# Raw weight chunks from the common pool of 8 KB units, in a hybrid decoder layer

## The chip, the cores and the metric

The kernel runs on one core of one Trainium2 chip. Its time is device time in microseconds (us), the median of several runs. Five engines work beside each other, each on its own list of instructions in a fixed order: TensorE (PE) for matmuls and transposes, VectorE (DVE), ScalarE (ACT), GpSimd (POOL), and SyncE (SP), which here only issues DMAs. They wait for each other through semaphores. "PEld" in the profile is TensorE's loading of weights, "PEclk" the clock that TensorE was granted, as a share of full speed.

## The reference

One decoder layer on x of 512 x 1024, everything in float32: a mixer with dilated attention (8 heads) and retention (4 heads) side by side, cross attention to 256 memory rows (4 heads), and SwiGLU. Each part is normed ahead and behind and added to x:

```
y = hybrid_mixer(rms_norm(x, pre_mix_g), w_in, attn_gn_g, ret_gn_g, w_out)
x = x + rms_norm(y, post_mix_g)
y = memory_cross_attn(rms_norm(x, pre_mem_g), mem, mem_norm_g, w_q, w_kv, w_o)
x = x + rms_norm(y, post_mem_g)
y = swiglu(rms_norm(x, pre_ffn_g), w_gate_up, w_down)
x = x + rms_norm(y, post_ffn_g)
```

where `rms_norm(x, g) = x * rsqrt(mean(x*x) + 1e-6) * g`, row by row. All the projections together read some 80 MB of weights.

## The kernel before

**Three matmuls for one.** A float32 product is computed from a high and a low half of each operand (`mm3`, L84 to L86): high by high, high by low, low by high. A weight therefore passes through four steps, in `load` (from L101): SP issues the DMA of a raw chunk of 128 x 2048 floats (8 KB in each partition, 1 MB in all; L109), ScalarE rounds it to the high half `wh` (L90), VectorE subtracts to get the low half `wl` (L91), each in two pieces of 1024 columns; then TensorE may use it. The tile names in the profile are `raw`, `wh`, `wl`. `split` does the same with activations.

**Chunks in a fixed sequence.** `chunks` lists all weight chunks in the order of use; `take` hands one out and calls `load` for those up to two ahead. For the mixer's output projection (`w_out`) and for the query projection of the cross attention (`w_q`) all four chunks are taken before the loop that uses them.

**Buffers.** `up` is a pool of 20 units of 8 KB (in each partition), all with one tag: the halves of weights, the transposed activations, queries, keys, values and x itself come from it through `unit` and `pair`. A new unit waits until the unit whose place it takes has had its last reader. `rawp` is a pool of two more units of 8 KB, for raw chunks alone, and for two landings of the memory input (`memTr`, L514, and `mrow`, L523): the third raw chunk waits until the first has been read out by ScalarE and VectorE. Gains that are multiplied along a row (`load_gain`, L168) come from a pool of two with tag `g`.

**Order.** The program is written once, as one stream of calls. A scheduler of the framework then gives each engine its own order, from priorities, from its own estimate of durations and from the release of buffers; so a change of the pools can move instructions on any engine, although none of them is written elsewhere. SP's list is in order too: a DMA that waits for its buffer holds up every DMA behind it.

**The places that matter here.** The first projection computes retention's queries and keys (`rqk`); beside it the root mean square of x is computed, and `bcast_row` (L175 to L177: `diag` on VectorE, `bc` on TensorE, `rbc` on VectorE) spreads it over the partitions for the rotation tables (`rope`, L242, on GpSimd) and the rotation (`t`, L245 to L247). Then retention's values (`rv`) follow. After the mixer, `residual` (L616 to L630) computes for a block of 128 rows a sum of squares on ScalarE (`junk`, L624), `pv` (L625), `z` (L626), a reciprocal root by three Newton steps (`pry`, `prw`, L137 to L141) and the new `x` (L630); `normed` does likewise and ends with `h` (L635). For the last block of four (b = 3) the small steps run on GpSimd, for the others on VectorE. The rows `h` are transposed on TensorE (`tp`) into `hh`, and `query` multiplies them with `w_q`: 8 groups of 24 matmuls for the first two row blocks, two groups to a chunk. After the cross attention the same chain makes `h3` for SwiGLU (`tp` at L792), whose gate and up projections are named `g` and `u`, the down projection `dn`.

Of the kernel before, what the change touches and what calls it, by code (L numbers as in the profile page):

```python
# [11 lines left out]
F32 = mybir.dt.float32  # L12
# [7 lines left out]
P = 128  # L20
D = 1024
S = 512
NM = 256
KT = D // P
# [14 lines left out]
def hybrid_layer(ctx, tc, t, out):  # L39
    nc = tc.nc  # L40
    cp = ctx.enter_context(tc.tile_pool(name="cp", bufs=1))
    up = ctx.enter_context(tc.tile_pool(name="up", bufs=20))
    rawp = ctx.enter_context(tc.tile_pool(name="rawp", bufs=2))
    wk = ctx.enter_context(tc.tile_pool(name="wk", bufs=4))
    sm = ctx.enter_context(tc.tile_pool(name="sm", bufs=4))
    psp = ctx.enter_context(tc.tile_pool(name="psp", bufs=8, space=bass.MemoryType.PSUM))
# [3 lines left out]
    def uname(p):  # L50
        cnt[0] += 1
        return f"{p}{cnt[0]}"
# [4 lines left out]
    def unit(name, dt=F32):  # L57
        return up.tile([P, 2048], dt, tag="u", name=uname(name))

    def pair(name):  # L60
        return unit(name + "h", F32R), unit(name + "l", F32R)
# [17 lines left out]
    def part(pr, c0, n):  # L79
        return pr[0][:, c0:c0 + n], pr[1][:, c0:c0 + n]  # L80
# [7 lines left out]
    def split(src, hi, lo, scale=None):  # L88
        if scale is None:
            nc.scalar.copy(hi, src)  # L90
            nc.vector.tensor_sub(lo, src, hi.bitcast(F32))  # L91
        else:
            nc.scalar.mul(hi, src, scale)
            nc.vector.scalar_tensor_tensor(lo, src, scale, hi.bitcast(F32), op0=ALU.mult, op1=ALU.subtract)

    chunks = [(name, i) for name, idx in (
        ("w_in", range(14)), ("w_kv", range(8)), ("w_out", (2, 3, 0, 1)), ("w_q", range(4)), ("w_o", range(4)),
        ("w_gu", range(FT)), ("w_dn", range(FT // 2))) for i in idx]
    loaded = {}

    def load(pieces=1, swap=False):  # L101
        key = chunks.pop(0)
        src = t[key[0]][key[1]]
        raw = rawp.tile([P, 2048], F32, tag="raw", name=uname("raw"))
        w = pair("w")
        n = 2048 // pieces
        for i in range(pieces):
            c = slice(i * n, (i + 1) * n)
            nc.sync.dma_start(raw[:, c], src[:, c])  # L109
        n = 2048 // max(2, pieces)  # L110
        for i in range(max(2, pieces)):
            c = slice(i * n, (i + 1) * n)
            if swap and i == 0:
                nc.vector.tensor_copy(w[0][:, c], raw[:, c])
                nc.vector.tensor_sub(w[1][:, c], raw[:, c], w[0][:, c].bitcast(F32))
            else:
                split(raw[:, c], w[0][:, c], w[1][:, c])
        loaded[key] = w

    def take(name, i, ahead=2):  # L120
        while (name, i) not in loaded:
            load()
        while chunks and len(loaded) - 1 < ahead:
            load()
        return loaded.pop((name, i))

    def ahead(name, i):
        while (name, i) in chunks:
            load()
# [20 lines left out]
    def row_rstd(rows, n, width, name, eps=EPS, e=None):  # L150
        ss = small([P, n], name + "s")
        for i, r in enumerate(rows):
            nc.scalar.activation(junk()[:, :width], r, AF.Square, accum_out=ss[:, i:i + 1])
        v = small([P, n], name + "v")
        (e or nc.vector).tensor_scalar(v, ss, 1.0 / width, eps, op0=ALU.mult, op1=ALU.add)
        return rsqrt(v, n, name, e)

    def load_rows(name):
        x = [unit("x") for _ in range(2)]
        for i in range(2):  # L160
            nc.sync.dma_start(x[i].rearrange("p (b d) -> p b d", b=2),
                              t["x"][i * 256:(i + 1) * 256, :].rearrange("(b p) d -> p b d", p=P))
        return [x[b // 2][:, (b % 2) * D:(b % 2 + 1) * D] for b in range(TB)]
# [7 lines left out]
    def bcast_row(col, n, dst):  # L171
        ps = bank("bc")
        for b in range(n):
            dg = wk.tile([P, P], F32, tag="diag", name=uname("diag"), bufs=1)
            nc.vector.tensor_scalar_mul(dg, ident, col[:, b:b + 1])  # L175
            nc.tensor.matmul(ps[:, b * P:(b + 1) * P], lhsT=ones, rhs=dg, start=True, stop=True)
        nc.vector.tensor_copy(dst, ps[:, :n * P])  # L177

# [1 line left out]
    gT = cp.tile([P, 3, KT], F32, name="gT")  # L180
    nc.scalar.dma_start(gT, t["gT"])
    hT = [pair("hT") for _ in range(2)]
# [24 lines left out]
    x = load_rows("x")  # L207
# [41 lines left out]

    w_rqk.clear()  # L250

# [1 line left out]
    def tok_proj(c0, name, evict):  # L253
        ws = []

        def one(b):
            if b == 0:
                ws[:] = [take("w_in", c0, 1), take("w_in", c0 + 1, 2)]
            ps = bank(name)
            for k in range(KT):  # L260
                mm3(ps, hx(k, b * P, P), part(ws[k // 4], (k % 4) * 512, 512), k == 0, k == KT - 1)
            if b == TB - 1:
                ws.clear()
            evict(b, ps)

        return [lambda b=b: one(b) for b in range(TB)]
# [33 lines left out]
            nc.tensor.transpose(ps[:, b * P:(b + 1) * P], src[:, c:c + P], ident)  # L300
        split(ps, *yx(k, 0, S), gT[:, 2, k:k + 1])

# [1 line left out]
    off = [0, 512, 1024, 896]  # L304
    inn, key, state = {}, {}, {}

# [58 lines left out]
    def ret_out(h):  # L365
        y_transposed(rg, 4 + h)

# [1 line left out]
    qk = [unit("qk", F32R) for _ in range(4)]  # L369
    kl = unit("kl", F32R)  # L370
    av = unit("av")
# [46 lines left out]
    def evict_av(b, ps):  # L418
        nc.scalar.mul(av[:, b * 512:(b + 1) * 512], ps, rstd0[:, b:b + 1])

# [1 line left out]
    scale = AD ** -0.5  # L422
    poff = [512 + 384, 1024, 512, 0]
    sbank = [(2, 0), (2, 256), (1, 0), (0, 0)]
# [82 lines left out]
    def att_out(pr):  # L507
        y_transposed(ya, pr)

# [1 line left out]
    mem = {}  # L511

    def mem_prepare():
        raw = rawp.tile([P, KT, NM], F32, tag="raw", name=uname("memTr"))  # L514
        nc.sync.dma_start(raw, t["memT"])
        m = pair("memT")
        for k in range(KT):
            split(raw[:, k, :], *part(m, k * NM, NM), gT[:, 1, k:k + 1])
        mem["T"] = m
        mem["k"], mem["v"] = pair("kT"), pair("vm")  # L520

    def mem_stats():
        mrow = rawp.tile([P, 2, D], F32, tag="raw", name=uname("mrow"))  # L523
        nc.sync.dma_start(mrow, t["mem"].rearrange("(b p) d -> p b d", p=P))
        mem["r"] = row_rstd([mrow[:, b, :] for b in range(2)], 2, D, "rm")
        mem["bc"] = cp.tile([P, NM], F32, name="mbc")
        bcast_row(mem["r"], 2, mem["bc"])
# [48 lines left out]
    att_scores(1)  # L576
    avs[3]()
    mem_prepare()
    fill = [lambda f=f: mem_keys(f) for f in range(8)] + [lambda c=c, b=b: mem_values(c, b) for c in range(2) for b in range(2)]

# [5 lines left out]
    for i in range(AH):  # L586
# [10 lines left out]
        if i % 3 == 2:  # L597
            filler()
        att_values(i)
# [1 line left out]
    x = load_rows("x")  # L601
    g1 = load_gain("post_mix_g")
    ret_out(0)
# [197 lines left out]
    to_h3(ha, 1)  # L801
    hc = mem_block(3)

# [1 line left out]
    af = []  # L805

    def gx(k, c0, n):
# [166 lines left out]
```

## Time and profile before

| | before |
|---|---|
| median of 3 runs | 829.76 us (829.33 to 831.52) |
| profiled execution, its span | 828.5 us |
| granted TensorE clock, mean | 0.991 |
| PE busy | 807.9 us, 98%, 4108 matmuls |
| DVE, ACT, POOL busy | 396.6, 305.4, 132.8 us |
| DMA over the span | 85.86 MB, 104 GB/s |

For the profiled execution no time is given beside its span. Times in the timeline are us from the start of the span; "x4" behind a row means that four equal instructions are merged into it, and the bracket behind a row gives the idle time of the engine ahead of it and what ended it.

### The profile page before, as it was taken

To read this page: it belongs to the slowest core of one execution; us is meant where nothing else is said; L and a number is where in the kernel's file an instruction comes from. 1 tells how busy PE (TensorE), PEld (TensorE's weight loads), DVE (VectorE), ACT (ScalarE), POOL (GpSimd) and SP (SyncE) were. 2 spreads that over 40 slices of the span, in tenths; PEclk is the share of its full clock that TensorE was granted. 3 is DMA by queue.
4 is the path that set the end of the run, shared out by engine and by line. 5 is a ranking of instruction groups with operands and counts; after the bars stand their busy time and mean duration, and the time that the engine had idled before them with its cause. 6 is when DMAs were issued, how large, how long until landed. Compare 5 with 4: busy or idle time off the path is not lost. (4 is left out here: it accounts for less than half of the span.)

```text
span 828.5 us, 10220 instructions
## 1 busy us (share of the span) xinstructions
PE 807.9 (98%) x4108; PEld 675.7 (82%) x4108; DVE 396.6 (48%) x766; ACT 305.4 (37%) x537; POOL 132.8 (16%) x176
## 2 busy tenths in 40 slices
PE   9979999999999999999999899999999999999996
PEld 7768888877777878999988788888888888888884
DVE  5595168764565657758446441405050314222144
ACT  5504333466464733445435232222130305332110
POOL 0161024410110100300036300000000004236000
PEclk9998999999999999999999999999999999999998
DMA  8726212221124440524002340505050322521011
GB/s 305 291 77 236 94 51 87 73 95 52 51 70 175 163 153 0 197 109 153 1 1 102 127 153 1 203 1 203 1 203 1 121 82 74 182 102 51 1 51 51
DMA packets 15519, 85.86 MB, mean 104 GB/s; under 512 B 1904, under 2 KB 1904, under 8 KB 6896
## 3 DMA queue, kind: packets, MB, share of 16 engines
q1 hardware_dynamic: 14752, 84.16, 27.7%
q10 hardware_dynamic: 720, 1.06, 0.3%
q8 instruction: 32, 0.52, 0.3%
q14 instruction: 15, 0.12, 0.0%
HBM read 83.11 MB, written 2.10 MB: 103 GB/s over the span
## 5 line engine op out<-in xcount | busy, mean ns | idle before, releaser
L91 DVE TENSOR_TENSOR wl<-raw,wh 128x1024 fp32r<-128x1024 f32 (+1 forms) x135 | 166.5, 1267 | 102.6 <-ACT wh L90 70.2
L90 ACT CAST wh<-raw 128x1024 fp32r<-128x1024 f32 (+1 forms) x135 | 133.8, 1042 | 95.3 <-DMA raw<-in_w_in 38.1
L820 DVE TENSOR_TENSOR af<-sg,u 128x512 f32<-128x512 f32 x22 | 15.1, 686 | 133.7 <-PE u L86 133.7
L846 POOL TENSOR_TENSOR al<-af,ah 128x512 fp32r<-128x512 f32 x22 | 34.6, 1605 | 257.5 <-ACT ah L845 243.3
L84 PE MATMUL g<-h3h,wh 128*128 128x512 f32 (+1 forms) x192 | 72.1, 375 | 0.0
L84 PE MATMUL u<-h3h,wh 128*128 128x512 f32 (+1 forms) x192 | 71.7, 373 | 0.0
L85 PE MATMUL g<-h3l,wh 128*128 128x512 f32 (+1 forms) x192 | 71.3, 371 | 0.0
L86 PE MATMUL g<-h3h,wl 128*128 128x512 f32 (+1 forms) x192 | 71.3, 371 | 0.0
L85 PE MATMUL u<-h3l,wh 128*128 128x512 f32 (+1 forms) x192 | 71.3, 371 | 0.0
L86 PE MATMUL u<-h3h,wl 128*128 128x512 f32 (+1 forms) x192 | 71.3, 371 | 0.0
L84 PE MATMUL dn<-wh,ah 128*128 128x512 f32 x176 | 68.5, 389 | 0.0
L85 PE MATMUL dn<-wl,ah 128*128 128x512 f32 x176 | 68.5, 389 | 0.0
L86 PE MATMUL dn<-wh,al 128*128 128x512 f32 x176 | 68.5, 389 | 0.0
L817 ACT ACTIVATE sg<-g 128x512 f32<-128x512 f32 x22 | 13.1, 598 | 149.2 <-PE g L86 123.0
L84 PEld LDWEIGHTS g<-h3h,wh 128*128 128x128 f32 x192 | 36.5, 190 | 6.5 <-ACT h3h L90 0.2
L84 PEld LDWEIGHTS u<-h3h,wh 128*128 128x128 f32 x192 | 36.6, 191 | 6.3
L85 PEld LDWEIGHTS g<-h3l,wh 128*128 128x128 f32 x192 | 36.2, 188 | 6.4
L86 PEld LDWEIGHTS g<-h3h,wl 128*128 128x128 f32 x192 | 36.2, 188 | 6.2
L85 PEld LDWEIGHTS u<-h3l,wh 128*128 128x128 f32 x192 | 36.2, 188 | 6.2
L86 PEld LDWEIGHTS u<-h3h,wl 128*128 128x128 f32 x192 | 36.1, 188 | 6.1
L84 PEld LDWEIGHTS dn<-wh,ah 128*128 128x128 f32 x176 | 33.0, 188 | 6.9
L86 PEld LDWEIGHTS dn<-wh,al 128*128 128x128 f32 x176 | 33.0, 188 | 6.9
(267 smaller groups left out, 1752.8 us busy)
## 6 DMA issues: line engine op xcount, KB each, us to landing
raw<-in_w_gu SPq DMA_DIRECT2D x22, 1024.0 KB, 4.8
raw<-in_w_in SPq DMA_DIRECT2D x12, 1024.0 KB, 5.1
raw<-in_w_dn SPq DMA_DIRECT2D x11, 1024.0 KB, 4.7
raw<-in_w_kv SPq DMA_DIRECT2D x8, 1024.0 KB, 4.7
x<-in_x SPq DMA_DIRECT2D x4, 1024.0 KB, 10.2
raw<-in_w_out SPq DMA_DIRECT2D x4, 1024.0 KB, 5.3
raw<-in_w_q SPq DMA_DIRECT2D x4, 1024.0 KB, 5.3
raw<-in_w_o SPq DMA_DIRECT2D x4, 1024.0 KB, 4.7
```

Source lines behind the costliest of these rows:

```text
L84: nc.tensor.matmul(o, lhsT=sh, rhs=mh, start=start, stop=False)
L85: nc.tensor.matmul(o, lhsT=sh, rhs=ml, start=False, stop=False)
L86: nc.tensor.matmul(o, lhsT=sl, rhs=mh, start=False, stop=stop)
L90: nc.scalar.copy(hi, src)
L91: nc.vector.tensor_sub(lo, src, hi.bitcast(F32))
L817: nc.scalar.activation(sg, pg, AF.Silu)
L820: nc.vector.tensor_mul(af[-1][:, (f % 4) * S:(f % 4 + 1) * S], sg, pu)
L846: nc.gpsimd.tensor_sub(lo[:, c], af[i][:, c], hi[:, c].bitcast(F32))
```

## The change

The pool `rawp` is gone. Raw chunks, `memTr` and `mrow` are units of `up` like everything else, and `up` has 23 units in place of 20 (two landing buffers and 20 units were 22). [...] The comment lines that were blanked and the line that fell away shift line numbers behind L42 by one: L109 of before is L108 of after, and tile numbers are lower by three.

```diff
-    up = ctx.enter_context(tc.tile_pool(name="up", bufs=20))
-    rawp = ctx.enter_context(tc.tile_pool(name="rawp", bufs=2))
+    up = ctx.enter_context(tc.tile_pool(name="up", bufs=23))
...
     def load(pieces=1, swap=False):
         key = chunks.pop(0)
         src = t[key[0]][key[1]]
-        raw = rawp.tile([P, 2048], F32, tag="raw", name=uname("raw"))
+        raw = unit("raw")
         w = pair("w")
...
     def mem_prepare():
-        raw = rawp.tile([P, KT, NM], F32, tag="raw", name=uname("memTr"))
+        raw = unit("memTr").rearrange("p (k s) -> p k s", k=KT)
         nc.sync.dma_start(raw, t["memT"])
...
     def mem_stats():
-        mrow = rawp.tile([P, 2, D], F32, tag="raw", name=uname("mrow"))
+        mrow = unit("mrow").rearrange("p (b d) -> p b d", b=2)
...
-    nc = _bacc.Bacc("TRN2", target_bir_lowering=False, num_devices=1)
+    nc = _bacc.Bacc("TRN2", target_bir_lowering=False, num_devices=1, dynamic_dma_scratch_size=1024)
```

The change moves instructions on SP, PE, DVE and ACT; GpSimd's order stays. Three places:

**SP at the start.** `raw` with `in_w_in` are chunks of the input projection; the first row here is chunk 2 before, and the second chunk 3. Before:

```order
L109 DMA raw_144<-in_w_in 128x2048
L109 DMA raw_156<-in_w_in 128x2048
L161 DMA x_152<-in_x 128x2x1024
L161 DMA x_153<-in_x 128x2x1024
L211 DMA rope_164<-in_rope 128x2048
```

After, the same place (behind the last load of `xraw`):

```order
L281 DMA zeta<-in_zeta 128x4
L283 DMA lmask<-in_lmask 128x512
L108 DMA raw_141<-in_w_in 128x2048
L167 DMA g_2231<-in_post_mix_g 128x1024
L167 DMA g_2447<-in_pre_mem_g 128x1024
L160 DMA x_149<-in_x 128x2x1024
L160 DMA x_150<-in_x 128x2x1024
L108 DMA raw_153<-in_w_in 128x2048
L210 DMA rope_161<-in_rope 128x2048
```

Chunk 3 (raw_153) stands behind both gains and both loads of x; before, it stood ahead of them. On PE the four `bc` matmuls of the same stage move from rows 122 to 131 of its list to rows 143 to 152.

**SP around the query projection.** The four chunks of `w_q`, the first two of `w_o`, and the gains `post_mem_g` and `pre_ffn_g`. Before:

```order
L109 DMA raw_2850<-in_w_q 128x2048
L109 DMA raw_2858<-in_w_q 128x2048
L109 DMA raw_2866<-in_w_q 128x2048
L109 DMA raw_2874<-in_w_q 128x2048
L109 DMA raw_3438<-in_w_o 128x2048
L168 DMA g_3470<-in_post_mem_g 128x1024
L109 DMA raw_3446<-in_w_o 128x2048
L168 DMA g_3682<-in_pre_ffn_g 128x1024
```

After:

```order
L108 DMA raw_2847<-in_w_q 128x2048
L108 DMA raw_2855<-in_w_q 128x2048
L167 DMA g_3467<-in_post_mem_g 128x1024
L108 DMA raw_2863<-in_w_q 128x2048
L167 DMA g_3679<-in_pre_ffn_g 128x1024
L108 DMA raw_2871<-in_w_q 128x2048
L108 DMA raw_3435<-in_w_o 128x2048
L108 DMA raw_3443<-in_w_o 128x2048
```

The gain `post_mem_g` now stands ahead of chunk 2 of `w_q`, `pre_ffn_g` ahead of chunk 3. Each takes the place of an older gain, and so waits until that one's last reader on VectorE is done.

**DVE around the query projection.** The low halves of chunks 0 to 3 of `w_q` and the residual of row blocks 2 and 3. Before, from the first block's second `z` on:

```order
L626 TENSOR_TENSOR z_2767<-o_2637,g_2234 128x512
L140 TENSOR_SCALAR prw_2778<-pry_2777,prn_2779 128x1
L91 TENSOR_TENSOR wl_2852<-raw_2850,wh_2851 128x1024
L141 TENSOR_SCALAR pry_2777<-prw_2778,pry_2777 128x1
L91 TENSOR_TENSOR wl_2852<-raw_2850,wh_2851 128x1024
L140 TENSOR_SCALAR prw_2778<-pry_2777,prn_2779 128x1
L91 TENSOR_TENSOR wl_2860<-raw_2858,wh_2859 128x1024
L141 TENSOR_SCALAR pry_2777<-prw_2778,pry_2777 128x1
L91 TENSOR_TENSOR wl_2860<-raw_2858,wh_2859 128x1024
```

After, from the end of that block's Newton chain, whose steps now follow each other without a break:

```order
L140 TENSOR_SCALAR pry_2774<-prw_2775,pry_2774 128x1
L629 SCALAR_TENSOR_TENSOR x_2228<-z_2764,pry_2774,x_2228 128x512
L629 SCALAR_TENSOR_TENSOR x_2228<-z_2764,pry_2774,x_2228 128x512
L90 TENSOR_TENSOR wl_2849<-raw_2847,wh_2848 128x1024
L90 TENSOR_TENSOR wl_2849<-raw_2847,wh_2848 128x1024
```

And after, from the `h` of that block on:

```order
L634 SCALAR_TENSOR_TENSOR h_2803<-x_2228,nry_2792,g_2447 128x1024
L625 TENSOR_TENSOR z_2806<-o_2635,g_2231 128x512
L625 TENSOR_TENSOR z_2806<-o_2636,g_2231 128x512
L629 SCALAR_TENSOR_TENSOR x_2228<-z_2806,pry_2816,x_2228 128x512
L629 SCALAR_TENSOR_TENSOR x_2228<-z_2806,pry_2816,x_2228 128x512
L90 TENSOR_TENSOR wl_2857<-raw_2855,wh_2856 128x1024
L90 TENSOR_TENSOR wl_2857<-raw_2855,wh_2856 128x1024
L634 SCALAR_TENSOR_TENSOR h_2845<-x_2228,nry_2834,g_2447 128x1024
L90 TENSOR_TENSOR wl_2865<-raw_2863,wh_2864 128x1024
```

The low half of chunk 0 (`wl_2849`) now follows the whole Newton chain and both writes of x; that of chunk 1 (`wl_2857`) follows the x of the next block, and that of chunk 2 its h.

## Prediction

> **What bounds the kernel now.** I read the page first, then the list of waits, then windows and the timeline around each hole in TensorE's work. The page says that TensorE is the bound:
>
> ```profile
> span 828.5 us, 10220 instructions
> PE 807.9 (98%) x4108; PEld 675.7 (82%) x4108; DVE 396.6 (48%) x766; ACT 305.4 (37%) x537; POOL 132.8 (16%) x176
> ```
>
> So only what opens or closes a hole in the PE row can move the end. The waits of PE and of SP's DMA queue (total, times, longest):
>
> ```profile
> PE rv L85 <- DVE wl L91: 5.2, 1, 5.2
> PE tp L792 <- DVE h L635: 4.0, 1, 4.0
> SPq L109 <- DVE wl L91: 532.2, 55, 54.3
> SPq L168 <- DVE z L626: 2.6, 2, 2.3
> ```
>
> PE has two real holes, 5.2 and 4.0 us. SP waits 532 us for a landing buffer to be read out by the low-half split of L91, which is the wait that this change removes; yet neither hole of PE is a wait for a DMA. Freeing that wait is therefore worth little by itself. Each hole also costs clock (windows; the stretch and its length, busy us of PE, PEld, DVE, ACT and POOL, granted clock, DMA):
>
> ```profile
> 59.45:62.86 3.41, 0.77 (x2) 0.68 (x3) 3.37 (x4) 0.00 (x0) 2.55 (x2) 0.50 0.00 0
> 465.64:469.05 3.41, 0.00 (x0) 0.00 (x0) 1.33 (x2) 0.00 (x0) 1.54 (x6) 1.00 0.00 0
> 469.05:472.47 3.42, 3.41 (x14) 3.09 (x15) 2.53 (x4) 1.97 (x3) 0.00 (x0) 0.50 0.00 0
> ```
>
> After the 3.41 us without any PE work the next such stretch has a granted clock of 0.50, and the first row shows the same inside the hole of 5.2 us.
>
> **The change, part by part.** The smaller DMA scratch: all DMAs of weights go over SP's queue, none over POOL's, so 0. The pool of 23 units: in the middle (70 to 285 us) and in SwiGLU (475 to 820 us) each raw chunk still has at least 10 us between the release of its unit and the first matmul that needs it, by the release and use times of this trace; also 0, hidden by PE's own work. What remains is the order of instructions, which the scheduler has rewritten on four engines. Four places matter.
>
> **1. Start (to 81 us): +1.** SP now sends zeta, lmask, both gains and both x loads ahead of chunk 3 (raw_153), and PE reaches the four bc matmuls at its row 143 instead of 122.
>
> ```profile
> 33.65 0.46 PE L176 MATMUL bc<-diag,ones 128*128 128x128 f32 x2 [0.30 <-DVE diag L175]
> 37.53 7.82 POOL L242 TENSOR_TENSOR rope<-rope,rbc 128x512 f32<-128x512 f32 x4 [36.10 <-DVE rbc L177]
> 40.73 1.78 DVE L245 TENSOR_TENSOR t<-sc,rope 128x512 f32<-128x512 f32 x1
> 45.93 0.69 DVE L245 TENSOR_TENSOR t<-rqk,rope 128x512 f32<-128x512 f32 x1
> 60.81 5.71 DVE L91 TENSOR_TENSOR wl<-raw,wh 128x1024 fp32r<-128x1024 f32 x4
> 56.54 0.39 PE L84 MATMUL rv<-wh,hTh 128*128 128x512 f32 x1
> 62.09 0.79 PE L85 MATMUL rv<-wl,hTh 128*128 128x512 f32 x1 [5.16 <-DVE wl L91]
> ```
>
> The bc matmuls follow 19 more 128x512 matmuls at about 0.23 us each: about 38.0 instead of 33.65. Everything behind them shifts by 4.3 us: POOL's rope pieces from 37.53 to 41.85, the first three t operations, slow beside POOL, from 40.73 to about 44, their end from 45.93 to about 49. Then come the 21 fast ones (45.93 to 60.81, 0.71 us each) and, now among them, the low half of chunk wl_282 (2 x 1.22), which used to run ahead of them. The low half that PE waits for began at 60.81 and now begins at about 66.6; its first 1024 columns end at about 67.9 instead of 62.0. But PE has 46 rv matmuls in front of it in place of 22: 24 x 0.227 = 5.4 us more work, so it stalls at about 62.0 instead of 56.5, for 5.9 instead of 5.5 us. Bounds: +2 if POOL and the slow t operations cost their full price again; -5.5 if the chain on DVE slips less than PE's added 5.4 us, since then nobody is late. I take +1, because every one of the delaying operations has its row.
>
> **2. Output projection: +0.5.** The first pv of the last row block, which waits for a ScalarE statistic, now stands in front of the end of a Newton chain on DVE; h for the next transposes comes about 0.5 us late.
>
> ```profile
> 322.54 0.15 DVE L625 TENSOR_SCALAR pv<-ps 128x1 f32<-128x1 f32 x1 [1.19 <-ACT junk L624]
> ```
>
> Bounds 0 and 1.2, the idle time that DVE shows ahead of that pv.
>
> **3. Queries (331 to 355 us): +5.5.** Here the change is dear. PE's side is 192 matmuls, 48 for each of the four chunks of w_q; from the first L86 to the last:
>
> ```profile
> 331.73 0.28 PE L86 MATMUL q<-hhh,wl 128*128 128x256 f32 x1
> 354.41 0.28 PE L86 MATMUL q<-hhh,wl 128*128 128x256 f32 x1
> ```
>
> That is 0.12 us for one and 5.76 for a chunk, so the first L86 of the chunks stands at 331.73, 337.49, 343.25 and 349.01. It needs the chunk's low half from DVE, where the order was:
>
> ```profile
> 312.14 1.28 DVE L626 TENSOR_TENSOR z<-o,g 128x512 f32<-128x512 f32 x2
> 315.25 1.42 DVE L630 SCALAR_TENSOR_TENSOR x<-z,pry,x 128x512 f32<-128x512 f32 x2
> ...
> 328.63 0.68 DVE L626 TENSOR_TENSOR z<-o,g 128x512 f32<-128x512 f32 x1
> 329.41 1.22 DVE L91 TENSOR_TENSOR wl<-raw,wh 128x1024 fp32r<-128x1024 f32 x1
> 331.98 1.22 DVE L91 TENSOR_TENSOR wl<-raw,wh 128x1024 fp32r<-128x1024 f32 x1
> 334.93 1.41 DVE L630 SCALAR_TENSOR_TENSOR x<-z,pry,x 128x512 f32<-128x512 f32 x2
> 342.94 1.28 DVE L626 TENSOR_TENSOR z<-o,g 128x512 f32<-128x512 f32 x2
> 345.84 1.42 DVE L630 SCALAR_TENSOR_TENSOR x<-z,pry,x 128x512 f32<-128x512 f32 x2 [1.62 <-POOL pry L141]
> 352.61 1.28 DVE L635 SCALAR_TENSOR_TENSOR h<-x,nry,g 128x1024 f32<-128x1024 f32 x1 [3.08 <-POOL nry L141]
> ```
>
> *Chunk 0.* Its split stood between the steps of the Newton chain; now it follows the whole chain and both x. In the undisturbed chain of the block before, z's end to x's end is 3.25 us (313.42 to 316.67). Here z ends at 329.3, x 332.6 to 333.1, first half 333.8 to 334.3. PE, shifted by 0.5, wants it at 332.2: stall 1.7.
>
> *Chunk 1.* Its split now follows the second x, which waits for POOL's pry and for z.
>
> ```profile
> 340.79 0.92 POOL L625 TENSOR_SCALAR pv<-ps,pv 128x1 f32<-128x1 f32 x1 [0.73 <-ACT junk L624]
> ```
>
> The first x ends at 333 in place of 336.3, and no cast stands between the statistics that follow it: the second pv starts at about 335.6 and x 4 to 5 us behind it (340.79 to 345.84 before), at 339.6 to 340.6. z ends at about 340.1, without the two splits that stood ahead of it. So x ends near 341 and the first half near 342.2. PE wants it at 339.7: stall 2.5.
>
> *Chunks 2 and 3.* SP issues in order, and the two gain loads now stand ahead of them:
>
> ```profile
> 331.91 2.90 SPq L109 DMA_DIRECT2D raw<-in_w_q  x2
> 344.25 0.33 SPq L168 DMA_DIRECT2D g<-in_post_mem_g  x1
> 353.92 0.33 SPq L168 DMA_DIRECT2D g<-in_pre_ffn_g  x1
> raw<-in_w_q SPq DMA_DIRECT2D x4, 1024.0 KB, 5.3
> ```
>
> The gain post_mem_g waits for the second z (344.25 is when z ended, 344.2) and pre_ffn_g for the h after it (353.92, h ended 353.9). So chunk 2, issued at 331.9 before, goes out at about 340.3 and lands at 345.6; cast and split (about 1.2 each, with what stands between) put its low half at 348, where PE arrives at 347.9: 0.2. Chunk 3 goes out behind h, at about 347.4, lands at 353, has its high half at 354 and its low half at 355.3; PE is there at 353.6: 1.1 to 1.5. Sum 1.7 + 2.5 + 0.2 + 1.1 = 5.5. Bounds: +2 (chunk 1 in time because pry is early, chunk 3's landing hidden) and +10 (each link of the serial chain z, pry, h, DMA, cast, split 1 us later than I put it, since chunk 3 adds all of them up). I take the middle, because the last three links have measured durations. None of these stalls empties a whole stretch of 3.41 us, as the one quoted above did, so I add no clock; if two of them cost a stretch at half clock, it would be 2 x 1.7 = 3.4 us more.
>
> **4. Stall at 464.8: -1.5.**
>
> ```profile
> 454.59 4.62 DVE L91 TENSOR_TENSOR wl<-raw,wh 128x1024 fp32r<-128x1024 f32 x4
> 454.73 2.26 POOL L625 TENSOR_SCALAR pv<-ps,pv 128x1 f32<-128x1 f32 x1 [0.61 <-ACT junk L624]
> 458.19 1.08 POOL L138 TENSOR_SCALAR prn<-pv 128x1 f32<-128x1 f32 x1
> 465.05 0.21 POOL L138 TENSOR_SCALAR nrn<-nrv 128x1 f32<-128x1 f32 x1
> 464.76 0.28 PE L86 MATMUL u<-h3h,wl 128*128 128x256 f32 x1
> 469.06 1.97 PE L792 MATMUL tp<-ident,h 128*128 128x128 f32 x8 [4.02 <-DVE h L635]
> ```
>
> Two of those four splits and their casts now stand behind h. The ScalarE statistic loses a cast in front of it (1.0 us), and POOL's L138 is 0.21 us rather than 1.08 where no split runs beside it: h and the transposes about 1.8 us sooner, at 467.25. One split then stands between h and the h3l of L85, which gives 0.9 of it back. The clock decides the rest: 0.9 to 2.7; both ends are kept, the value is near the middle. [...]
>
> **Sum:** 828.5 + 1 + 0.5 + 5.5 - 1.5 = 834.0 us of span. The median of the runs lies 1.3 us above the profiled span (829.76 against 828.5), so 835.3 us.
>
> **The rivals.** *No change.* The queries cost only their lower bound, +2, and 4. gives -2.7: 828.5 + 1 + 0.5 + 2 - 2.7 = 829.3, or 830.6 timed. For it: PE hides whatever is early, and chunk 1 has only 2.5 us of stall to lose. Against it: SP's order, since chunk 3 cannot be sent before h. *Faster.* The place is the start: DVE's chain slips by less than PE's added 5.4 us, the hole at 56.5 closes, -5.5; with 4. at -2.7 and the queries at +2: 828.5 - 5.5 + 0.5 + 2 - 2.7 = 822.8, or 824.1. It decides from the point where the low half ends before 62.0. Against it: bc moved by 4.3 us and the chain behind it has no idle time on DVE from 40.7 to 62. *Much slower.* The serial chain of the queries at its upper bound with two stretches at half clock: 834.0 + 4.5 + 3.4 = 841.9, or 843.2; for it speaks that four dependent chunks arrive late one behind the other.
>
> **How the numbers follow.** Forecast (+3 to +10 us) 0.60, much slower 0.12, no change 0.15, faster 0.13. A measurement of this kernel can tell 0.3%, 2.5 us, from no change; so faster 0.13, same 0.15, slower 0.72. The range 828 to 842.5 takes in the no-change case and nearly the much slower one; below it lies most of the faster case. The forecast's own range is 832 to 840.
>
> **What would show it.** In the changed trace: PE waits for wl of L90 at about 62 us for nearly 6 us; in the query stage two waits of q's third pass for wl, of about 1.7 and 2.5 us, and a wait of q's first pass for wh of chunk 3; SP's DMA queue shows post_mem_g, chunk 2, pre_ffn_g, chunk 3 from 340 to 347.5 us; the last q matmul at about 361 us instead of 354.4; tp's wait for h down from 4.0 to about 2.5. If chunks 2 and 3 land before PE asks for them, step 3 is wrong; if the wait near 62 us is absent, step 1 is.

## The result, and the profile after

| | before | after |
|---|---|---|
| median of 4 runs each, same chip | 829.61 us (829.33 to 831.52) | 841.90 us (839.75 to 843.71) |
| ratio of the times | | 1.0144, interval 1.0124 to 1.0164 |
| profiled execution, its span | 828.5 us | 839.6 us |
| granted TensorE clock, mean | 0.991 | 0.989 |

The change makes the kernel slower, by 12.3 us in the medians and by 11.1 us in the profiled spans. The forecast had 5.5 us. The page of after:

```profile
span 839.6 us, 10208 instructions
PE 812.0 (97%) x4108; PEld 677.9 (81%) x4108; DVE 396.7 (47%) x766; ACT 304.5 (36%) x537; POOL 125.9 (15%) x176
```

The number of matmuls is the same, and DVE and ACT do the same amount of work. What is longer is the idle time of PE. Its waits after (total, times, longest):

```profile
PE rv L84 <- DVE wl L90: 5.7, 1, 5.7
PE q L85 <- DVE wl L90: 4.6, 3, 2.8
PE tp L791 <- DVE h L634: 2.6, 1, 2.6
PE bc L175 <- DVE diag L174: 1.6, 2, 1.2
PE otr L489 <- ACT ot L481: 1.3, 1, 1.3
```

Before, only the first and third of these were there (5.2 and 4.0 us), and 0.9 us of `bc`. To see where the time is lost, the same matmul is looked up in both timelines: the end of the start (`inn`), the transposes ahead of the queries (first `tp`), those behind the first half of the queries (second `tp`), and the last down projection (`dn`). Before:

```profile
98.27 1.05 PE L313 MATMUL inn<-rqT,rkT 128*128 128x128 f32 x8
324.28 1.91 PE L643 MATMUL tp<-ident,h 128*128 128x128 f32 x16
354.53 1.91 PE L643 MATMUL tp<-ident,h 128*128 128x128 f32 x16
820.28 0.39 PE L86 MATMUL dn<-wh,al 128*128 128x512 f32 x1
```

After:

```profile
99.28 1.05 PE L312 MATMUL inn<-rqT,rkT 128*128 128x128 f32 x8
327.92 1.04 PE L642 MATMUL tp<-ident,h 128*128 128x128 f32 x8
330.02 1.09 PE L642 MATMUL tp<-ident,h 128*128 128x128 f32 x8 [0.83 <-DVE h L634]
367.11 1.91 PE L642 MATMUL tp<-ident,h 128*128 128x128 f32 x16
831.41 0.39 PE L85 MATMUL dn<-wh,al 128*128 128x512 f32 x1
```

After lags by 1.01, 3.64, 12.58 and 11.13 us at these four. Between the first and the second the mixer has lost 2.63 us, which the prediction had put at nothing. Between the second and the third 8.94 us go, about 1.05 of them at the transposes (the wait of 0.83 us and the list of eight breaking in two) and 7.89 in the queries. Behind the third 1.45 us come back: 0.38 at the transposes behind the queries, 0.25 on the way to the hole near 465 us, and 0.82 at that hole (its wait is 1.42 us shorter, and 0.6 us are lost again right behind it).

**The mixer.** One place in it, told by one tile: the two statistics of `mrow` on ScalarE, and the DMA that brings `mrow` (first and last start). Before:

```profile
L153 ACT ACTIVATE junk<-mrow x2: 1050/1054/1059, 81.5 to 82.7; 128x1024 bf16<-128x1024 f32 x2
L524 SPq DMA_DIRECT2D mrow<-in_mem x1: 378/378/378, 75.7 to 75.7; - x1
```

After, with what follows from it on DVE and PE:

```profile
L152 ACT ACTIVATE junk<-mrow x2: 1057/1059/1061, 101.5 to 102.7; 128x1024 bf16<-128x1024 f32 x2
L523 SPq DMA_DIRECT2D mrow<-in_mem x1: 379/379/379, 74.1 to 74.1; - x1
108.50 1.23 DVE L90 TENSOR_TENSOR wl<-raw,wh 128x1024 fp32r<-128x1024 f32 x1 [1.36 <-ACT wh L89]
109.64 0.28 DVE L174 TENSOR_SCALAR diag<-ident,rmy 128x128 f32<-128x128 f32 x1
109.98 0.49 PE L175 MATMUL bc<-diag,ones 128*128 128x128 f32 x2 [1.18 <-DVE diag L174]
```

The data come 1.6 us sooner, but the statistics stand 20 us later in ScalarE's list. The Newton chain behind them on DVE then ends so late that the second `diag` falls behind a low half, which in turn waits 1.36 us for its cast. PE waits 1.2 us. The second such place is `otr` at 269 us, where ScalarE's list has a `vf`, which waits 6.17 us for PE's `mv`, ahead of the copy `ot` that PE needs:

```profile
268.01 0.69 ACT L547 ACTIVATE vf<-mv,rmy 128x512 f32<-128x512 f32 x1 [6.17 <-PE mv L85]
268.59 0.58 ACT L481 COPY ot<-oT 128x512 f32<-128x512 f32 x1
269.22 0.66 PE L489 MATMUL otr<-ident,ot 128*128 128x128 f32 x4 [1.31 <-ACT ot L481]
```

No transfer is late in either place. What is late is an instruction in a list that an engine works through in order. PE's waits between `inn` and the first `tp` add up to 3.2 us in place of 1.2; the remaining 0.6 of the 2.63 us is not told apart here.

**The queries.** PE's waits in this stage, in their order (the first is for chunk 0 of `w_q`, the second for chunk 1, the last two for chunk 3):

```profile
338.11 0.39 PE L85 MATMUL q<-hhh,wl 128*128 128x256 f32 x1 [1.27 <-DVE wl L90]
346.89 0.58 PE L85 MATMUL q<-hhh,wl 128*128 128x256 f32 x1 [2.76 <-DVE wl L90]
360.48 0.39 PE L83 MATMUL q<-hhh,wh 128*128 128x256 f32 x1 [0.98 <-ACT wh L89]
361.74 0.38 PE L85 MATMUL q<-hhh,wl 128*128 128x256 f32 x1 [0.52 <-DVE wl L90]
```

They add up to 5.53 us. The windows around the second (the stretch and its length, busy us of PE, PEld, DVE, ACT and POOL, granted clock, DMA) show what it costs besides:

```profile
343.09:346.50 3.41, 1.04 (x9) 0.84 (x7) 2.83 (x5) 0.70 (x1) 0.87 (x3) 1.00 0.45 123
346.50:349.91 3.41, 3.02 (x14) 3.02 (x15) 1.47 (x2) 0.45 (x2) 2.34 (x6) 0.50 0.88 336
```

Here the stretch in which PE was busy for 1.04 of 3.41 us is followed by one at a granted clock of 0.50. PE works for 3.02 us of that one, so by an estimate from this row (half of 3.02) it costs about 1.5 us. With the 5.53 this makes 7.0 of the 7.89 us; the rest lies in the matmuls right behind the four holes. What DVE had ahead of chunk 1's low half, and SP's queue with the casts that follow it:

```profile
344.29 1.41 DVE L629 SCALAR_TENSOR_TENSOR x<-z,pry,x 128x512 f32<-128x512 f32 x2 [0.58 <-POOL pry L140]
345.62 2.35 DVE L90 TENSOR_TENSOR wl<-raw,wh 128x1024 fp32r<-128x1024 f32 x2
343.73 0.33 SPq L167 DMA_DIRECT2D g<-in_post_mem_g  x1
344.15 0.38 SPq L108 DMA_DIRECT2D raw<-in_w_q  x1
352.37 0.33 SPq L167 DMA_DIRECT2D g<-in_pre_ffn_g  x1
352.75 0.43 SPq L108 DMA_DIRECT2D raw<-in_w_q  x1
350.62 2.00 ACT L89 CAST wh<-raw 128x1024 fp32r<-128x1024 f32 x2 [3.67 <-DMA raw<-in_w_q]
359.39 2.00 ACT L89 CAST wh<-raw 128x1024 fp32r<-128x1024 f32 x2 [6.77 <-DMA raw<-in_w_q]
```

Each of the last two chunks goes out right behind a gain and is cast 6.5 and 6.6 us after its issue (344.15 to 350.62, 352.75 to 359.39). So the two waits for chunk 3, 1.50 us together, are in the end waits for a transfer, which SP's order sent late.

### The profile page after: what moved, and what is told of

Same layout as the page of the kernel before. It is cut to its first block, busy times and chain, and to the rows that moved or that the text cites. A ratio compares the mean times of both kernels' runs of the same rounds, so it can differ in the third digit from the quotient of the medians.

```text
span 839.6 us, 10208 instructions
## 1 busy us (share of the span) xinstructions
PE 812.0 (97%) x4108; PEld 677.9 (81%) x4108; DVE 396.7 (47%) x766; ACT 304.5 (36%) x537; POOL 125.9 (15%) x176
## 4 chain that ended last, share of the span: by engine, by line
PE 52%; DVE 4%; POOL 3%; issue 2%; DMA 1%; ACT 1%; DVEq 0%; SPq 0%; POOLq 0%; ACTq 0%
PE dn L85 5%; PE dn L83 5%; PE dn L84 5%; PE g L84 5%; PE g L85 5%; PE u L85 5%; PE u L84 5%; PE u L83 4%; PE g L83 4%; PE o L83 1%; PE o L85 1%; PE o L84 1%; PE q L85 1%; PE q L83 1%; PE q L84 1%
## 5 line engine op out<-in xcount | busy, mean ns | idle before, releaser
L845 POOL TENSOR_TENSOR al<-af,ah 128x512 fp32r<-128x512 f32 x22 | 31.2, 1452 | 254.4 <-ACT ah L844 247.9
L85 PE MATMUL q<-hhh,wl 128*128 128x256 f32 x128 | 36.5, 291 | 4.6 <-DVE wl L90 4.6
L84 PEld LDWEIGHTS dn<-wl,ah 128*128 128x128 f32 x176 | 33.1, 188 | 6.9
```

The lines of the kernel that those rows point to most:

```text
L84: nc.tensor.matmul(o, lhsT=sh, rhs=ml, start=False, stop=False)
L85: nc.tensor.matmul(o, lhsT=sl, rhs=mh, start=False, stop=stop)
L845: nc.gpsimd.tensor_sub(lo[:, c], af[i][:, c], hi[:, c].bitcast(F32))
```

## The experiments

Four theories stood against each other. **Order:** the loss is the new order of the lists of SP, DVE and ACT. **Units:** it is the pool, raw chunks and halves taking buffers from each other. **Scratch:** the argument `dynamic_dma_scratch_size=1024` costs time. **Landing room:** more raw chunks under way change the time by themselves. Differences are those of medians to the kernel before on the same chip.

**The scratch alone.** The kernel before, with one argument more; the order of its instructions stays.

```diff
-    nc = _bacc.Bacc("TRN2", target_bir_lowering=False, num_devices=1)
+    nc = _bacc.Bacc("TRN2", target_bir_lowering=False, num_devices=1, dynamic_dma_scratch_size=1024)
```

> Before with the 1 KB descriptor scratch and nothing else; every engine's order is that of before. Theory A (the loss is the new order of instructions): same as before, 829 to 831 us, ratio within 0.3% of 1. Rival C (the smaller scratch slows the DMAs): part of the 12 us shows here, and the median time of a weight chunk from issue to landing grows above 4.7 to 5.3 us.

Measured: 830.14 against 830.15 us, ratio 1.0002 (0.9993 to 1.0012). The scratch costs nothing that can be measured.

**Landing room alone.** The same, and a third landing buffer.

```diff
-    rawp = ctx.enter_context(tc.tile_pool(name="rawp", bufs=2))
+    rawp = ctx.enter_context(tc.tile_pool(name="rawp", bufs=3))
```

> The memory that the change takes from the scratch, used otherwise: 20 units as before and a landing pool of three 8 KB buffers in place of two. The order on PE, DVE and ACT stays nearly that of before; on SP the two late gains go behind the loads of the output weights. Theory A (the loss of the change is its order on DVE and SP, not the number of buffers, and the landing wait of before hides under PE): no change, 828 to 831 us, although one more chunk may land ahead. If landing room itself is worth something: 827 us or less. Rival B has no say here.

Measured: 829.87 against 829.96 us, ratio 0.9992 (0.9983 to 1.0001). A half more room to land in is worth nothing that can be measured. It does not take SP's wait away: SP waits 523.4 us for low halves here, and 532.2 us before. What a kernel without that wait would do in the old order, no run shows.

**One unit less in the pool.** The change with 22 units, as many as before had in all. The order on the engines is that of the change.

```diff
-    up = ctx.enter_context(tc.tile_pool(name="up", bufs=23))
+    up = ctx.enter_context(tc.tile_pool(name="up", bufs=22))
```

> The change with 22 units in place of 23; the order on all five engines is that of the change. Theory A: the time of the change, 840 to 844 us, ratio about 1.014, since the order decides and the unit more or less does not. Rival B (raw chunks now wait for units, the pool is too tight): one unit fewer makes it slower, 845 us or more, with longer waits of PE for wh.

Measured: 844.63 against 830.15 us, ratio 1.0176 (1.0161 to 1.0191), a little above the change, and just above the 840 to 844 us that the theory of order allowed. The order on SP, PE, DVE and ACT is that of the change, as expected. Its waits for weights in the queries are no longer than with 23: 4.2 us for `wl` and 0.8 for `wh`, where the change has 4.6 and 1.0. So the theory of units falls. The profiled span is 3.3 us above that of the change (842.9 against 839.6), at a mean granted clock of 0.985 against 0.989; by an estimate (842.9 x 0.015 less 839.6 x 0.011 us, at 0.5 x 3.41 us each) that is two more stretches at half clock. One stands behind a wait of `bc` in the mixer, which is 1.83 us here (the change had 0.4 and 1.2):

```profile
109.90 0.49 PE L175 MATMUL bc<-diag,ones 128*128 128x128 f32 x2 [1.83 <-DVE diag L174]
107.31:110.72 3.41, 1.58 (x14) 1.39 (x14) 2.30 (x3) 2.02 (x3) 0.33 (x1) 1.00 0.17 70
110.72:114.13 3.41, 3.41 (x11) 2.64 (x10) 3.10 (x19) 0.00 (x0) 0.00 (x0) 0.50 0.02 5
```

Two times 1.7 us is about the difference. Why the two waits of `bc` fell together is open.

**SP's order alone.** 22 units, and the three later gains in a buffer class of their own, so that they need not wait for older gains. Only SP's list changes.

```diff
-    def load_gain(name):
-        g = wk.tile([P, D], F32, tag="g", name=uname("g"), bufs=2)
+    def load_gain(name, tag="g", bufs=2):
+        g = wk.tile([P, D], F32, tag=tag, name=uname("g"), bufs=bufs)
...
-    g3 = load_gain("post_mem_g")
+    g3 = load_gain("post_mem_g", "g2", 3)
```

> 22 units, and the three late gains (post_mem, pre_ffn, post_ffn) have buffers of their own, so that none waits for an older gain; SP then has no gain between the chunks of the query projection, and the order of PE, DVE, ACT and POOL is that of the change. If SP's blocked queue costs what the trace of the change shows for chunks 2 and 3 (waits of q for wh of 1.0 us and for the last wl of 0.7 us): 1.8 us less than the run before it, the waits for chunks 0 and 1 (1.4 and 2.8 us) stay. If the blocked queue is the main part of the query stage's loss (as the prediction's step 3 has it for chunks 2 and 3, or more): 4 us less or better. If SP's order does not matter: no difference.

Measured: 839.87 against 830.15 us, ratio 1.0123 (1.0107 to 1.0140); 4.8 us below its own base with 22 units. The wait for `wh` is gone, that for `wl` is not (4.3 us in three waits, the longest 2.4). So in the query stage the stalls fall from 5.0 (4.2 and 0.8) to 4.3 us, by 0.7 us.

The profiled span is 5.6 us below that of 22 units. By the mean granted clocks, 0.989 against 0.985, some 3.4 us of this is clock, an estimate (842.9 x 0.015 less 837.3 x 0.011). The order on PE, DVE, ACT and POOL is the same in both runs, and so is the hole of chunk 1 (2.41 and 2.40 us); with the gains of their own the granted clock is 1.00 over this hole and behind it (342.00 to 348.80 us). In the start and the mixer 2.8 us are gained, 1.6 of them at 110 us, where the same wait of `bc` has no half clock behind it:

```profile
108.73 0.49 PE L175 MATMUL bc<-diag,ones 128*128 128x128 f32 x2 [1.83 <-DVE diag L174]
104.80:108.21 3.41, 2.10 (x16) 1.79 (x14) 1.24 (x2) 2.56 (x3) 1.00 (x1) 1.00 0.55 231
108.21:111.62 3.41, 2.89 (x16) 2.51 (x17) 3.34 (x14) 0.00 (x0) 0.00 (x0) 1.00 0.02 5
```

By its size the gain would fit the branch of the expectation that makes SP's queue the main part (4 us or better); the stalls do not bear that out. SP's order is shown to be worth 0.7 us of stalls, less than the 1.8 us expected; what part of the other 4 us belongs to it, these runs do not show. The stalls that remain in the queries are DVE's order.

**Chunks of `w_q` first.** The change, with the four `take` calls at a higher priority in the scheduler.

```diff
-    wq = [take("w_q", c, 0) for c in range(4)]
+    with tc.high_priority():
+        wq = [take("w_q", c, 0) for c in range(4)]
```

> The change with the loads of the four query chunks given priority in the scheduler. On SP chunk 2 goes ahead of post_mem and chunk 3 ahead of pre_ffn; on DVE the low half of chunk 1 goes ahead of the second z of the last block and so of the x that waits for POOL; that of chunk 0 stays behind both x. Theory A: the wait for chunk 0 stays at 1.4 us, that for chunk 1 falls from 2.8 to below 1 us and with it the half-clock stretch behind it (1.7 us); chunk 3 no longer waits: 835 to 838 us. Rival B: no change from 842 us.

Measured: 843.08 against 830.15 us, ratio 1.0158 (1.0143 to 1.0173); a miss. DVE and PE in the stage:

```profile
350.97 1.28 DVE L634 SCALAR_TENSOR_TENSOR h<-x,nry,g 128x1024 f32<-128x1024 f32 x1 [4.56 <-POOL nry L140]
352.17 2.35 DVE L90 TENSOR_TENSOR wl<-raw,wh 128x1024 fp32r<-128x1024 f32 x2
353.44 0.39 PE L85 MATMUL q<-hhh,wl 128*128 128x256 f32 x1 [4.06 <-DVE wl L90]
```

Chunk 1's wait fell from 2.76 to 0.16 us. But its split now stands between the two `z`, the chain of the last block ends no sooner, and chunk 2's low half, which stands behind that chain's `h`, is late by 4.06 us. The theory of order was put too narrowly: it isn't the place of one chunk that counts. A low half is late when it stands behind a waiting step of the residual chain, whichever chunk it is.

**Two chunks of `w_q` taken early.** The change, with the loads of the first two chunks of `w_q` written ahead of the output projection and its residuals, and given priority. In the trace their splits fall into the Newton chains of earlier blocks (at 312.88 and 319.81 us).

```diff
+    with tc.high_priority():
+        ahead("w_q", 1)
     hs0 = mix_half(0)
```

> The change with the loads of the first two query chunks written ahead of the output projection and given priority. On SP all four query chunks then go ahead of both gains, and on DVE no low half of a query chunk stands behind the x that waits for POOL or behind the last h. Theory A, as mended by the run before (in the query stage some low half stands behind a wait of DVE, whichever chunk it is): the waits of q for wl and wh, together 5.6 us, fall below 1 us and the half-clock stretch behind them goes; 6 to 8 us less than the change, 834 to 837 us. If the pool is what makes the chunks late: the waits stay, 840 us or more.

Measured: 833.25 against 829.96 us, ratio 1.0034 (1.0020 to 1.0049), 9 us better than the change (3.3 above before, where that was 12.3). Of PE's waits in the query stage only two of 0.3 us for `hhh` are left. The order of this one stage is thus the larger part of the loss, and a two-line edit that leaves the pool alone brings it back.

**The start, in both kernels.** One chunk more of `w_in` is loaded ahead of the rotation, so that its low half stands earlier on DVE, in the kernel before and in the change, with the same edit.

```diff
-    ahead("w_in", 4)
+    ahead("w_in", 5)
```

> Before with the second chunk of the retention values loaded where the first one is, ahead of the rotation, so that on DVE its low half stands behind the second t operation in place of the last. The wait of 5.2 us at 56.5 us goes, and with it the half clock behind it (about 2 us): 821 to 824 us. If the wait only moves (the rotation then ends about 2.5 us later and PE waits for it): 826 us or more.

> The change with the same edit at the start as in the run before last: the low half of the second chunk of the values moves from behind the last t operation to behind the sixth. The wait of 5.7 us at 61 us falls to below 2 us, and one of the half-clock stretches behind it goes: 5 to 8 us less than the change, 834 to 837 us.

Measured: before with it 822.63 against 829.96 us, ratio 0.9913 (0.9891 to 0.9935); the change with it 835.93 us, ratio 1.0072 (1.0049 to 1.0094). The wait of `rv` falls from 5.2 to nothing and from 5.7 to 1.1 us, and the kernels gain 7.3 and 6.3 us, more than the wait. Clock comes back with it: the mean granted clock of the profiled executions is 0.996 in place of 0.991 and 0.993 in place of 0.989, and in the kernel before with the edit it is 1.00 from 59 to 76 us, where it was 0.50 from 59.45 to 66.28. The hole of both kernels at the start is the same thing and not the change's.

**Both repairs of the change together.**

> The change with both edits of the runs before: the query chunks written early and the second chunk of the values loaded ahead of the rotation. If the two losses are separate, their gains add: 841.9 - 8.7 - 6.0 = 827.2 us, and against before there remain the two waits of the mixer (bc 1.6, otr 1.3) less the shorter wait at 465. If they are one loss (the later stage only passes on what the start cost), less: 832 us or more.

Measured: 828.40 against 829.70 us, ratio 0.9979 (0.9969 to 0.9990). Against their kernels before, the two repairs alone gained 9.0 and 6.3 us, and both together 13.6 us: the gains add up but for 1.7 us, about one stretch of 3.41 us at half clock by the estimate of 0.5 x 3.41.

**All repairs at once, by priorities.** On the change with both repairs: `mem_stats()` moved ahead of `ret_inner(0)`, the first four chunks of `w_gu` taken early, the last block's small steps on VectorE. On the kernel before: the start and the same three edits, with the chunks of `w_gu` one block later.

```diff
+    mem_stats()
     ret_inner(0)
...
-        residual(out_proj((b,), o_lhs, wo, nat, "o2", 0, mid)[b], b, g3, nc.gpsimd)
-        return normed(b, g4, nc.gpsimd)
+        e = nc.vector if b == 3 else nc.gpsimd
+        residual(out_proj((b,), o_lhs, wo, nat, "o2", 0, mid)[b], b, g3, e)
+        return normed(b, g4, e)
...
     h = mem_block(0, lambda: x_transposes(3))
+    with tc.high_priority():
+        ahead("w_gu", 3)
     x_values(1)
```

> On top of that: the memory statistics written ahead of the first retention step, the first four chunks of w_gu written ahead of the cross attention's second half and given priority, and the last row block's residual and norm on DVE in place of GpSimd. The bc wait of 1.6 us and the tp wait of 2.6 us with its half-clock stretches (up to 3.4 us) go: 820 to 823 us. If the GpSimd chain was not what made h late, the tp wait stays: 825 us or more.

> The same edits on before, with its two fixed landing buffers (the w_gu chunks written one block later; no edit of the query loads, whose order needs none there). Against the run of before with the edit at the start alone (822.6 us) the tp wait of 4.0 us and its half-clock stretch (1.7 us) go: 816 to 819 us. If it comes out at the time of the pool's version with these edits, the pool costs nothing in itself; if 3 us or more below it, the order in the mixer (otr) still costs there. If the fixed landing buffers hold the four w_gu chunks back, 820 us or more.

Measured: the change with them 841.74 against 829.70 us, ratio 1.0143 (1.0126 to 1.0160); before with them 825.69 us, ratio 0.9955 (0.9943 to 0.9967), less gained than by the start alone. Both missed. In the first, PE's waits and DVE ahead of the larger one:

```profile
PE o L83 <- DVE oTxl L90: 10.7, 1, 10.7
PE bc L175 <- DVE diag L174: 5.5, 1, 5.5
427.62 4.62 DVE L90 TENSOR_TENSOR wl<-raw,wh 128x1024 fp32r<-128x1024 f32 x4
432.16 2.74 DVE L90 TENSOR_TENSOR oTxl<-xo,oTxh 128x256 fp32r<-128x256 f32 x8
```

The early splits of `w_gu` pushed the `oTxl` that PE needed next behind themselves. And moving `mem_stats` brought the `bc` matmuls forward on PE (to 91.6 us) further than the chain of statistics that they need, so that their longest wait grew from 1.2 to 5.5 us. Here an order moved by priority made larger holes than those it closed.

**The last hole, by taking work out of its way.** The kernel before with the start of above, and in the loop over the first two chunks of `w_gu` only one chunk taken ahead for f = 0 and none for f = 1 (two each before), so that none of these chunks' low halves stands ahead of the last `z` on DVE.

```diff
-    ahead("w_in", 4)
+    ahead("w_in", 5)
...
-        w, pg, pu = take("w_gu", f), bank("g"), bank("u")
+        w, pg, pu = take("w_gu", f, 1 - f), bank("g"), bank("u")
```

> Before with the edit at the start, and with only two chunks of w_gu loaded ahead of the last norm in place of four: the four low halves that stood on DVE ahead of the last row block's second z go behind h, and nothing else moves on DVE, ACT and PE but what follows from it. If these splits are what makes the last h late (by holding z and by slowing GpSimd's chain beside them, as step 4 of the prediction has it): h comes about 4 us sooner, the tp wait of 4.0 us falls below 0.5 and its half-clock stretch goes, 816 to 818 us. If the GpSimd chain itself is too long: the wait stays above 2 us, 820 us or more.

Measured: 817.50 against 830.28 us, ratio 0.9849 (0.9832 to 0.9865), faster than both kernels, and 5.1 us below the start alone. The second `z` of the last block follows the first without a split between them:

```profile
446.43 1.28 DVE L626 TENSOR_TENSOR z<-o,g 128x512 f32<-128x512 f32 x2
...
455.97 1.29 DVE L635 SCALAR_TENSOR_TENSOR h<-x,nry,g 128x1024 f32<-128x1024 f32 x1 [4.58 <-POOL nry L141]
```

Apart from the first microsecond (`warm`) PE has no wait left above 0.6 us.

**The same for the change.** Both repairs, the edit of `w_gu`, and four buffers for `diag` in place of one.

```diff
-            dg = wk.tile([P, P], F32, tag="diag", name=uname("diag"), bufs=1)
+            dg = wk.tile([P, P], F32, tag="diag", name=uname("diag"), bufs=4)
```

> The change with both earlier edits (828.4 us), the same edit on w_gu, and four buffers for the diagonal tile of the broadcast in place of one, so that the two diagonals of the memory statistics follow each other on DVE and no low half stands between them. If the first part of the mixer's loss is that low half: the bc wait falls from 1.6 us to below 0.7. With the tp wait of 2.6 us and its two half-clock stretches gone as well: 821 to 824 us. What then remains above the run of before with the same edits is the otr wait (1.3 us) and the ret copies (0.7 us). If the memory statistics are late for another reason, the bc wait stays.

Measured: 821.48 against 830.28 us, ratio 0.9895 (0.9881 to 0.9910). The wait of `bc` is down from 1.6 to 0.4 us; `otr` with 1.3, `g` with 1.1 and `ro` with 0.7 us remain, and `tp` with 0.7. With these repairs the version with two fixed landing buffers is still 4.0 us faster than that with the common pool. These four waits add up to 3.8 us and are all for DVE and ACT, so what is left of the difference again has the look of order; no run closed it.

## Why the prediction was right in direction and wrong in size

**What bounds the kernel: right.** Holes in PE's row and the clock behind them are what moved. SP's wait for landing buffers was worth nothing to PE: in the change SP waits 117.7 us for `wl` in place of 532.2 (and 173.1 us for PE's `u`, a new wait for units), and of PE's two holes only that near 465 us became shorter, with the order on DVE and ACT. The 0 for the scratch came out (830.14 against 830.15 us with it alone); why it costs nothing, no run shows.

**Step 1, the start (+1): the parts right, the sum lucky.** `bc` ran at 38.00, the low half came from 66.14 on, and PE waited 5.7 us for it where 5.9 was said; the lag is 1.01 us. But the working of this step, a stall of 5.9 in place of 5.5 us, gives 0.4 us, and the +1 that was taken is not worked out. In the traces the wait grew by 0.6 us (5.16 to 5.72). The stretches at a granted clock of 0.50 behind it, which end at 66.28 before and at 73.43 after, reach 4.2 and 6.0 us beyond the hole's end; half of the difference, about 0.9 us, is the estimate of what they cost more. Smaller waits of PE ahead of it are 0.5 us less. So the clock, which the step did not count, made the +1 come true.

**The middle at 0: the step that failed by kind.** It was argued from the release of units and the use of chunks, "at least 10 us between the release of its unit and the first matmul". No matmul waits for a chunk there in the changed trace either. But order on DVE and ACT had changed there too, and was not looked at: the stage lost 2.63 us, with `diag`, `ret` and `vf` ahead of `ot` behind its new waits. For `diag` the last experiment shows it (1.6 to 0.4 us with four buffers); for the other two it is read from the trace alone. The prediction named four places and left out the fifth.

**Step 2, the output projection (+0.5): 1.05 us**, inside its bounds of 0 and 1.2, but by another cause. The first `pv` of the last block stands where it was said, at 327.76, and waits for nothing there. What is late is the whole residual chain: ScalarE's first sum of squares, which waits for PE's `o`, starts at 310.67 in place of 299.96 us, and the `h` that PE needs ends at 329.96 in place of 321.34, 8.6 us later, where PE itself comes 3.6 us later.

**Step 3, the queries (+5.5): the stalls right, the clock wrong.** The four waits add up to 5.53 us: chunk 0 1.27 for 1.7, chunk 1 2.76 for 2.5, chunk 2 nothing for 0.2, chunk 3 1.50 for 1.1 to 1.5. SP's queue had the order that was said, 3.4 to 5.4 us later than said; 3.2 us of that came in with the stage, which PE reached 4.69 us late in place of 1.5. Chunk 3's stall came out right in part by luck: the chunk landed 6.6 us after its issue where 5.6 was reckoned, and PE, at half clock for a while, came later too. The step that failed here is "I add no clock": behind the hole of chunk 1 stands a stretch at a granted clock of 0.50, about 1.5 us by the estimate above, and the holes cost some 0.9 us more in the matmuls behind them. The stage cost 7.89 us. The reason given, that none of the stalls empties a whole stretch of 3.41 us, was not enough: the hole was 2.76 us, PE was busy for 1.04 us of the stretch, and the next ran at 0.50. The trace of before has such a row too, since the stretch ahead of its first one at 0.50 was not empty, with PE busy for 0.89 us:

```profile
56.04:59.45 3.41, 0.89 (x4) 0.39 (x3) 3.31 (x6) 0.00 (x0) 1.99 (x2) 1.00 0.00 0
```

**Step 4, the hole near 465 us (-1.5): -0.82.** The wait fell from 4.02 to 2.6 us as said (2.5), but only in part by the links that were named. The wait for ScalarE's statistic ahead of the second `pv` (0.61 us) went, as said; `prn` on POOL takes 1.08 us in both traces, and it is that `pv` itself that fell from 2.26 to 0.27 us. Right behind the hole 0.6 us are lost again, 0.3 of them in a wait for `h3l`. The clock gave nothing back: a stretch at 0.50 stands behind the hole of 2.6 us as well (after, windows):

```profile
476.20:479.62 3.42, 0.81 (x8) 0.61 (x6) 1.37 (x2) 1.60 (x3) 1.51 (x6) 1.00 1.01 412
479.62:483.03 3.41, 3.41 (x14) 2.89 (x14) 3.41 (x5) 2.00 (x3) 0.00 (x0) 0.50 0.48 202
```

**The sum.** 834.0 predicted, 839.6 measured: 2.6 from the middle, 2.4 from the queries' clock and refill, 0.5 from step 2 and 0.7 from step 4, less 0.6 at the transposes behind the queries and on the way to the hole. In all runs the time lies 1.8 us above the run's own span. The 1.3 us that the prediction added were less, because the profiled execution of before lay half a microsecond above its median; that of after lies as much below its own. This is the last microsecond of the miss.

**The rivals.** "Much slower", 843.2 us timed, came closest to 841.9, with one of its two clock stretches, but not for its reason: the serial chain stood near the middle of its bounds, and the mixer made up the rest. "Faster" fell where it said it would be decided, at the start: the low half was ready at 67.4, not before 62.0. Its other condition was met and does not do what was said: DVE's chain slipped by 5.33 us (60.81 to 66.14), less than 5.4, but a hole that was 5.16 us wide before does not close by that.

## What to carry to other kernels

When pools change under a scheduler that sets each engine's order, compare the order of every in-order list over the whole program and not only where buffers are tight: here the scratch, a third landing buffer and one unit less changed nothing that the waits show, and exchanged rows on DVE, ACT, SP and PE cost 12 us. A weight's split that stands behind a step of another chain on the same engine can be late by that chain's wait; here it was cured by taking the chunks earlier, or by taking them later and out of the way, and each priority that is raised has to be followed to what it pushes back. A hole of PE is priced with its clock: here stretches of 3.41 us at a granted clock of 0.50 stood behind holes of 1.83 to 5.72 us, up to 1.7 us each by the estimate of 0.5 x 3.41, and behind another hole of 1.83 us there was none.

## What the runs showed of the hardware that was not expected

**Short holes had half clock behind them, but not each of them.** Stretches at a granted clock of 0.50 were seen behind holes of 2.76 us (after, 346.50 to 349.91 us), of 2.6 us (after, 479.62 to 483.03) and of 1.83 us (22 units, 110.72 to 114.13). The one of 1.83 us shows that the length of a hole alone does not tell: with 22 units the next 3.41 us ran at 0.50, and with the gains of their own, behind the same wait, at 1.00 (110.82 to 114.20).

With 22 units PE was busy for 1.58 us of the stretch ahead of that at 0.50 (107.31 to 110.72); with the gains of their own the hole lay in two of the stretches shown, with 2.10 and 2.89 us (104.80 to 111.62). What made the difference between the two runs, they do not show. Busy is here what the profile shows, whose ends of matmuls are modelled, and all these kernels are variants of one.

**The same kernel had different clocks.** The four runs of after had spans of 837.9, 839.6, 840.6 and 841.9 us at mean clocks of 0.992, 0.989, 0.987 and 0.986: the longer, the lower. One stretch of 3.41 us at 0.50 lowers the mean clock by 0.5 x 3.41 / 840, or 0.002, and costs up to 1.7 us, so by this estimate the spread of 4 us is two to three stretches. The kernel without holes, 817.50 us, had a clock of 0.997 to 0.998 and a spread of 1.5 us.

**A chunk right behind another transfer landed late.** In the change 1 MB of `w_q` landed 6.4 and 6.6 us after its issue when a gain of 0.5 MB had gone out 0.4 us ahead. The first two chunks of `w_q`, issued at 295.30 and 317.01 us with no other transfer of SP's queue in the 5 us ahead, landed in 4.6 us each. The kernel before shows the same behind a chunk: the one issued at 331.91 us, with none in the 5 us ahead, landed in 4.8 us, and the next, 2.6 us behind it, in 6.0 us.
